# Fourteen matmuls on constants between the first and the second transposes of x

## The chip, the cores and the metric

The kernel runs on one core of one Trainium2 chip. The metric is the device time of one execution in microseconds (us). A core has five engines, each with a queue of its own that is worked off in order: TensorE (PE in the profile, with its weight loads as PEld), VectorE (DVE), ScalarE (ACT), GpSimd (POOL) and SyncE (SP), which only issues DMAs here. They wait for each other through semaphores.

## The reference

The reference is an encoder of two layers on 512 tokens of width 2048, with 16 learned tokens put ahead. Layer 0 is attention (16 query heads, 8 key and value heads, head width 128), layer 1 is gated linear attention in chunks. Each layer norms its input, projects it, mixes, gates, projects back, norms again and adds to the stream. For the change only the beginning matters:

```python
h = jnp.concatenate([meta, x], axis=1)
...
y = rmsnorm(h, pre_norm[i])
...
proj = h @ w_in
q, k, v, gate = jnp.split(
    proj, [ATTN_WIDTH, ATTN_WIDTH + ATTN_KV_WIDTH, ATTN_WIDTH + 2 * ATTN_KV_WIDTH], axis=-1)
```

All of it is in float32. The kernel reaches that precision by splitting each operand into a high and a low part and adding three products: high by high, low by high, high by low.

## The kernel before

x comes in with tokens on the partitions, and the projections need it with channels there. The kernel works in 16 steps of 128 channels, k = 0 to 15. `start_k(k)` (L441) makes one step ready: four transposes on TensorE into a PSUM tile `pt` (L444, one for each 128 tokens); on ScalarE the high part `uh`, scaled by the norm's weight (L445); on VectorE the low part `ul` (L446), which needs `uh`; and on ScalarE a copy `h0` of `pt` (L449), which GpSimd writes to memory (L450). There are two `pt` buffers, so the transposes of a step wait until the copy of an earlier one is done. From k = 4 on, `start_k` also squares pieces of x for the norm's sum, on ScalarE (L463, which writes its unused result over `pt`) and on VectorE (L466). A square on VectorE reads x alone, nothing that TensorE makes.

`meta()` (L426) does the same for the 16 learned tokens: 16 small transposes (L429), a copy (L431), a product (L434), a split.

`group` (L172) is the first projection: one key head and two query heads, each in two halves of 264 tokens, so six PSUM tiles. They are called `pp` (three of them) and `g3`, `g4`, `g5`. For every k each tile takes three matmuls: L155 (`uh` by `whi`), L156 (`ul` by `whi`), L157 (`uh` by `wlo`). For k = 0, 1, 2 it does the first half of the tokens first, then the second half, since that one needs the learned tokens.

The weights come as blocks of 128 x 1024 (`wraw`), two buffers in all, and are split by `weights` and `split` (L131 to L133): the high part `whi` on ScalarE (L132), the low part `wlo` on VectorE (L133). The first two blocks come in pieces; one piece is split on GpSimd (L384, L385). The next blocks are loaded by SyncE as a buffer comes free (L150). SyncE's queue also brings x: four pieces of 128 channels, then two of 256 and two of 512 (L369).

Ahead of it all stand 13 matmuls of a tile of ones by itself, on the tile `warm` (L401).

The order in which the engines' instructions stand is not the order of the code. A scheduler places them by estimates of when each can run, except for instructions held by `pin`, which keep their place among each other.

Of the kernel before, what the change touches and what calls it, by code (L numbers as in the profile page):

```python
# [19 lines left out]
P = 128  # L20
# [62 lines left out]
def hybrid_encoder(  # L83
# [6 lines left out]
    V, A, G, PE = nc.vector, nc.scalar, nc.gpsimd, nc.tensor  # L90
    clk = Clock()
    pin = tc.keep_in_program_order
# [26 lines left out]
    ones_r = const.tile([P, P], F32R, name="ones_r")  # L119
# [11 lines left out]
    def split(hi, lo, src):  # L131
        A.copy(hi, src)  # L132
        V.tensor_tensor(lo, src, hi.bitcast(F32), op=ALU.subtract)  # L133
# [234 lines left out]
    def load_x(c, n):  # L368
        nc.sync.dma_start(out=xt[:, :, c:c + n], in_=x_v[:, :, c:c + n])  # L369
# [9 lines left out]
    def split_w(i, k, m):  # L379
        raw, n = ((raw0, P), (raw1, 256))[i]  # L380
        c = slice(k * n, (k + m) * n)
        hi, lo = [t[:, c] for t in unit0[i, 0]]
        if i and k == 0:
            G.tensor_copy(hi, raw[:, c])  # L384
            G.tensor_tensor(lo, raw[:, c], hi.bitcast(F32), op=ALU.subtract)  # L385
        else:
            split(hi, lo, raw[:, c])
# [14 lines left out]
    accs, banks = [], []  # L402
# [18 lines left out]
    def load_rows():  # L421
        for src, r0, n in vec:
            flat = src.rearrange("a b c -> (a b c)") if len(src.shape) == 3 else src.rearrange("a b -> (a b)")
            nc.gpsimd.dma_start(out=rows[r0:r0 + n, :], in_=flat.rearrange("(r p) -> r p", p=P))

    def meta():  # L426
        mt = ps_t.tile([P, 512], F32, tag="t", name="mt")[:, :KT * META].rearrange("p (k m) -> p k m", m=META)
        for k in range(KT):
            PE.transpose(mt[:, k], xm[:, k * P:(k + 1) * P], ident[:META, :META])  # L429
        h0m = sp.tile([P, KT, META], F32, name="h0m")  # L430
        V.tensor_copy(h0m, mt)  # L431
        nc.gpsimd.dma_start(out=h0_d[:, :, SEQ:].rearrange("k p m -> p k m"), in_=h0m)
        um = sp.tile([P, KT, META], F32, name="um")
        V.tensor_tensor(um, h0m, pre0.unsqueeze(2).broadcast_to([P, KT, META]), op=ALU.mult)  # L434
        split(uh[:, :, SEQ:], ul[:, :, SEQ:], um)
# [5 lines left out]
    def start_k(k):  # L441
        pt = ps_t.tile([P, 512], F32, tag="t", name="pt")
        for t in range(4):
            PE.transpose(pt[:, t * P:(t + 1) * P], xs[t][:, k * P:(k + 1) * P], ident)  # L444
        A.activation(uh[:, k, :SEQ], pt, AF.Copy, scale=pre0[:, k:k + 1])  # L445
        V.scalar_tensor_tensor(ul[:, k, :SEQ], pt, pre0[:, k:k + 1], uh[:, k, :SEQ].bitcast(F32),  # L446
                               op0=ALU.mult, op1=ALU.subtract)
        h0 = s2.tile([P, SEQ], F32, tag="h0", name="h0", bufs=6)
        A.copy(h0, pt)  # L449
        nc.gpsimd.dma_start(out=h0_d[k][:, :SEQ], in_=h0)  # L450
        if k >= 4 and todo:
            square(*todo.pop(0), pt)
        if k >= 8 and todo:
            square(*todo.pop(0), None)
# [15 lines left out]
    def start(k, part):  # L470
        if part == 1:
            return
        for at, c, n in ((1, 768, 256), (3, 1024, 512), (6, 1536, 512)):
            if at == k:
                load_x(c, n)
        if k == 0:
            split_w(0, 0, 4)
            start_k(0)
            split_w(1, 0, 2)
            split_w(1, 2, 2)  # L480
        if k == 4:
            load_rows()
        if k == 2:
            split_w(0, 4, 4)
            meta()
        if k + 1 < KT:
            start_k(k + 1)
    group([(w_in0, 2048, P), (w_in0, 0, 256)], accs, start, 0, halves=3,
          units={(i, 0): [t.rearrange("p (k n) -> p k n", n=n) for t in unit0[i, 0]] for i, n in ((0, P), (1, 256))})
    ct = ps_t.tile([P, 512], F32, tag="t", name="ct")  # L490
# [1082 lines left out]
```

## Time and profile before

| | us |
|---|---|
| three runs | 1771.58, 1776.51, 1779.26 |
| median | 1776.51 |
| profiled execution | 1775.28 |
| its span, first to last instruction | 1773.4 |
| busy VectorE | 1150.9 |
| busy ScalarE | 991.6 |
| busy GpSimd | 389.0 |

The span leaves out 1.9 us around the instructions. Busy times say which engine is the fullest; what a change in one place is worth is read from the waits in that place. In the timelines below, a row has the start, the duration, the engine, the line, the operation, what it writes and reads (out<-in), the shapes, and in brackets how long the engine stood idle before it and what ended that. A row about DMA has the size and the median time from issue to landing.

### The profile page before, as it was taken

To read this page: it belongs to the slowest core of one execution; us is meant where nothing else is said; L and a number is where in the kernel's file an instruction comes from. 1 tells how busy PE (TensorE), PEld (TensorE's weight loads), DVE (VectorE), ACT (ScalarE), POOL (GpSimd) and SP (SyncE) were. 2 spreads that over 40 slices of the span, in tenths; PEclk is the share of its full clock that TensorE was granted. 3 is DMA by queue.
4 is the path that set the end of the run, shared out by engine and by line. 5 is a ranking of instruction groups with operands and counts; after the bars stand their busy time and mean duration, and the time that the engine had idled before them with its cause. 6 is when DMAs were issued, how large, how long until landed. Compare 5 with 4: busy or idle time off the path is not lost.

```text
span 1773.4 us, 31460 instructions
## 1 busy us (share of the span) xinstructions
PE 1733.7 (98%) x12379; PEld 1630.9 (92%) x12379; DVE 1150.9 (65%) x1799; ACT 991.6 (56%) x2032; POOL 389.0 (22%) x495
## 2 busy tenths in 40 slices
PE   8999999999999999999999999999999999999998
PEld 8999999999999999999999999998788889888886
DVE  5867775566566656786756976667677676763224
ACT  5545445666666665744457445447677685853222
POOL 3103201356456545331141001110010100000000
PEclk9999999999999999999999999999999999999999
DMA  8444434233333334464376344445333332444333
GB/s 255 139 126 133 129 120 125 77 112 109 85 107 100 109 85 110 151 198 121 110 244 176 117 138 120 120 118 143 84 112 93 102 96 78 123 126 175 95 95 130
DMA packets 273347, 220.98 MB, mean 125 GB/s; under 512 B 13324, under 2 KB 243408, under 8 KB 272672
## 3 DMA queue, kind: packets, MB, share of 16 engines
q1 hardware_dynamic: 253920, 158.76, 31.5%
q0 software_dynamic: 19280, 60.23, 10.3%
q8 instruction: 97, 1.59, 0.4%
q14 instruction: 50, 0.41, 0.1%
HBM read 177.92 MB, written 34.53 MB: 120 GB/s over the span
## 4 chain that ended last, share of the span: by engine, by line
PE 56%; DVE 4%; ACT 4%; DMA 2%; issue 1%; POOL 0%; DVEq 0%; POOLq 0%; ACTq 0%
PE pp L155 7%; PE pp L157 7%; PE pp L156 7%; PE pp L242 3%; PE pp L241 3%; PE pp L243 3%; PE f L1485 3%; PE f L1483 3%; PE f L1484 2%; PE px L243 2%; PE px L241 2%; PE px L242 2%; ACT whi L132 1%; DVE wlo L133 1%; PE o L1311 1%
## 5 line engine op out<-in xcount | busy, mean ns | idle before, releaser
L155 PE MATMUL pp<-uh,whi 128*128 128x264 f32 (+1 forms) x1744 | 549.1, 315 | 0.4 <-ACT y L888 0.3
L157 PE MATMUL pp<-uh,wlo 128*128 128x264 f32 (+1 forms) x1744 | 539.6, 309 | 1.4 <-DVE wlo L133 1.1
L156 PE MATMUL pp<-ul,whi 128*128 128x264 f32 (+1 forms) x1744 | 539.0, 309 | 2.1 <-DVE ul L446 2.1
L133 DVE TENSOR_TENSOR wlo<-wraw,whi 128x1024 fp32r<-128x1024 f32 (+1 forms) x222 | 282.5, 1273 | 234.0 <-ACT whi L132 233.3
L132 ACT CAST whi<-wraw 128x1024 fp32r<-128x1024 f32 (+1 forms) x222 | 231.3, 1042 | 273.7 <-PE f L1485 83.4
L157 PEld LDWEIGHTS pp<-uh,wlo 128*128 128x128 f32 x1744 | 329.1, 189 | 18.9 <-DVE wlo L133 1.6
L155 PEld LDWEIGHTS pp<-uh,whi 128*128 128x128 f32 x1744 | 329.1, 189 | 17.0 <-ACT uh L445 0.5
L156 PEld LDWEIGHTS pp<-ul,whi 128*128 128x128 f32 x1744 | 329.6, 189 | 16.0 <-DVE ul L446 2.6
L132 ACT CAST whi<-x 128x1024 fp32r<-128x1024 f32 x82 | 86.1, 1050 | 121.0 <-PE pp L242 70.9
L133 DVE TENSOR_TENSOR wlo<-x,whi 128x1024 fp32r<-128x1024 f32 x82 | 102.7, 1262 | 44.5 <-ACT whi L132 44.4
L241 PE MATMUL px<-uh,whi 128*128 128x264 f32 x320 | 91.3, 285 | 0.0
L243 PE MATMUL px<-uh,wlo 128*128 128x264 f32 x320 | 91.1, 285 | 0.0
L709 ACT ACTIVATE pn<-s,mx 128x528 f32<-128x528 f32 (+1 forms) x72 | 50.5, 701 | 72.1 <-DVE mx L706 72.1
L242 PE MATMUL px<-ul,whi 128*128 128x264 f32 x320 | 90.7, 283 | 0.0
L706 DVE TENSOR_REDUCE mx<-s 128x1 f32<-128x528 f32 (+1 forms) x72 | 50.8, 706 | 55.6 <-PE s L703 55.1
L1485 PE MATMUL f<-whi,ul 128*128 128x512 f32 x192 | 75.6, 394 | 0.0
L1483 PE MATMUL f<-whi,uh 128*128 128x512 f32 x192 | 75.6, 394 | 0.0
L1484 PE MATMUL f<-wlo,uh 128*128 128x512 f32 x192 | 75.4, 393 | 0.0
L314 POOL DMA_DIRECT2D qs<-qw x96 | 48.0, 506 | 98.7 <-ACT sq L308 76.6
L726 DVE TENSOR_TENSOR pl<-pT,ph 128x512 fp32r<-128x512 f32 (+1 forms) x80 | 47.5, 594 | 25.5 <-ACT ph L725 24.9
L242 PEld LDWEIGHTS px<-ul,whi 128*128 128x128 f32 x320 | 60.2, 188 | 0.0
L243 PEld LDWEIGHTS px<-uh,wlo 128*128 128x128 f32 x320 | 60.2, 188 | 0.0
(491 smaller groups left out, 4539.8 us busy)
## 6 DMA issues: line engine op xcount, KB each, us to landing
wraw<-in_gla_w_in_dram SPq DMA_DIRECT2D x77, 512.0 KB, 4.0
wraw<-in_attn_w_in_dram SPq DMA_DIRECT2D x75, 512.0 KB, 4.0
wraw<-in_gla_w_out_dram SPq DMA_DIRECT2D x32, 512.0 KB, 3.9
wraw<-in_attn_w_out_dram SPq DMA_DIRECT2D x23, 512.0 KB, 4.6
x<-in_attn_w_in_dram SPq DMA_DIRECT2D x19, 512.0 KB, 4.4
x<-in_gla_w_in_dram SPq DMA_DIRECT2D x19, 512.0 KB, 4.1
qs<-qw POOLq DMA_DIRECT2D x96, 66.0 KB, 3.5
g_d<-y POOLq DMA_DIRECT2D x20, 264.0 KB, 2.4
```

Source lines behind the costliest of these rows:

```text
L132: A.copy(hi, src)
L133: V.tensor_tensor(lo, src, hi.bitcast(F32), op=ALU.subtract)
L155: PE.matmul(ps, wh, uh[:, k, a:b], start=first, stop=False)
L156: PE.matmul(ps, wh, ul[:, k, a:b], start=False, stop=False)
L157: PE.matmul(ps, wl, uh[:, k, a:b], start=False, stop=last)
L241: PE.matmul(ps, w[0][:, k], bh[:, k], start=k == 0 and not more, stop=False, skip_group_check=more)
L242: PE.matmul(ps, w[0][:, k], bl[:, k], start=False, stop=False, skip_group_check=more)
L243: PE.matmul(ps, w[1][:, k], bh[:, k], start=False, stop=k == KH - 1, skip_group_check=more)
L706: V.reduce_max(mx, s, axis=AX.XY, negate=True)
L1483: PE.matmul(ps, uh[:, k, ts], wh[:, kk], start=(k == 0), stop=False)
L1484: PE.matmul(ps, uh[:, k, ts], wl[:, kk], start=False, stop=False)
L1485: PE.matmul(ps, ul[:, k, ts], wh[:, kk], start=False, stop=(k == KT - 1))
```

## The change

Behind the first step of `start_k`, fourteen matmuls of the tile of ones by itself are put, into the tile `g3` of the projection (`accs[-2]` after its sort). The first matmul of the projection on that tile starts its sum anew, so nothing of theirs is kept. `pin` keeps them in their place.

```diff
@@ -483,6 +483,9 @@
         if k == 2:
             split_w(0, 4, 4)
             meta()
+        if k == 0:
+            for _ in range(14):
+                pin(PE.matmul(accs[-2][0][:, :P], ones_r, ones_r, start=True, stop=True))
         if k + 1 < KT:
             start_k(k + 1)
```

On TensorE they stand between the transposes of k = 0 and those of k = 1. They also change the scheduler's estimates, and with them the order on ScalarE, VectorE and GpSimd up to about k = 7. SyncE's order is the same, and so are all orders behind that. Three places matter.

VectorE at k = 2, before. `ul` from `pt_196` is that of k = 2; the `junk` rows are squares of x, `h0m` and `um` belong to the learned tokens.

```order
L133 TENSOR_TENSOR wlo_121<-wraw_118,whi_120 128x512
L446 SCALAR_TENSOR_TENSOR ul_89<-pt_196,pre0_155,uh_88 128x512
L431 COPY h0m_234<-mt_217 128x256
L466 SCALAR_TENSOR_TENSOR junk_428,ssq_158<-xt_116 128x512
L434 TENSOR_TENSOR um_237<-h0m_234,pre0_155 128x256
L466 SCALAR_TENSOR_TENSOR junk_471,ssq_158<-xt_116 128x512
L446 SCALAR_TENSOR_TENSOR ul_89<-pt_241,pre0_155,uh_88 128x512
```

The same place now, where `pt_190` is k = 1, `pt_210` is k = 2 and `pt_255` is k = 3:

```order
L133 TENSOR_TENSOR wlo_121<-wraw_118,whi_120 128x512
L446 SCALAR_TENSOR_TENSOR ul_89<-pt_190,pre0_155,uh_88 128x512
L466 SCALAR_TENSOR_TENSOR junk_442,ssq_158<-xt_116 128x512
L466 SCALAR_TENSOR_TENSOR junk_485,ssq_158<-xt_116 128x512
L446 SCALAR_TENSOR_TENSOR ul_89<-pt_210,pre0_155,uh_88 128x512
L431 COPY h0m_248<-mt_231 128x256
L466 SCALAR_TENSOR_TENSOR junk_516,ssq_158<-xm_117 16x512
L434 TENSOR_TENSOR um_251<-h0m_248,pre0_155 128x256
L466 SCALAR_TENSOR_TENSOR junk_547,ssq_158<-xt_116 128x512
L446 SCALAR_TENSOR_TENSOR ul_89<-pt_255,pre0_155,uh_88 128x512
```

The first two squares of x have moved ahead of the `ul` of k = 2.

ScalarE at k = 5, before. `pt_288` is k = 4, `pt_329` is k = 5, `pt_358` is k = 6; `wraw_448` is the block of weights for k = 8 to 15 of the key head.

```order
L132 CAST whi_318<-wraw_317 128x1024
L445 ACTIVATE uh_88<-pt_329,pre0_155 128x512
L132 CAST whi_449<-wraw_448 128x1024
L449 COPY h0_336<-pt_329 128x512
L463 ACTIVATE pt_329,ssq_158<-xt_116 128x512
L445 ACTIVATE uh_88<-pt_358,pre0_155 128x512
```

And now, where `pt_255`, `pt_302`, `pt_343` and `pt_372` are k = 3 to 6, and `wraw_462` is the same block of weights:

```order
L132 CAST whi_332<-wraw_331 128x1024
L449 COPY h0_262<-pt_255 128x512
L449 COPY h0_309<-pt_302 128x512
L463 ACTIVATE pt_302,ssq_158<-xt_116 128x512
L132 CAST whi_463<-wraw_462 128x1024
L445 ACTIVATE uh_88<-pt_343,pre0_155 128x512
L449 COPY h0_350<-pt_343 128x512
L445 ACTIVATE uh_88<-pt_372,pre0_155 128x512
```

The split of that block has moved ahead of the `uh` of k = 5, and two copies of h have moved behind the split of the block ahead of it.

VectorE at k = 5, before:

```order
L466 SCALAR_TENSOR_TENSOR junk_601,ssq_158<-xt_116 128x512
L466 SCALAR_TENSOR_TENSOR junk_632,ssq_158<-xt_116 128x512
L446 SCALAR_TENSOR_TENSOR ul_89<-pt_329,pre0_155,uh_88 128x512
L466 SCALAR_TENSOR_TENSOR junk_663,ssq_158<-xm_117 16x512
L133 TENSOR_TENSOR wlo_450<-wraw_448,whi_449 128x1024
L446 SCALAR_TENSOR_TENSOR ul_89<-pt_358,pre0_155,uh_88 128x512
```

And now:

```order
L466 SCALAR_TENSOR_TENSOR junk_615,ssq_158<-xt_116 128x512
L466 SCALAR_TENSOR_TENSOR junk_646,ssq_158<-xt_116 128x512
L466 SCALAR_TENSOR_TENSOR junk_677,ssq_158<-xm_117 16x512
L133 TENSOR_TENSOR wlo_464<-wraw_462,whi_463 128x1024
L446 SCALAR_TENSOR_TENSOR ul_89<-pt_343,pre0_155,uh_88 128x512
L446 SCALAR_TENSOR_TENSOR ul_89<-pt_372,pre0_155,uh_88 128x512
```

The low part of the same weights has moved ahead of the `ul` of k = 5.

## The prediction

> **What bounds the kernel now.** I read the busy times first, then the table of clock and busy time by window, then what TensorE (PE) waits for in the first 45 us, then the timeline of each engine there.
>
> ```profile
> span 1773.4 us, 31460 instructions
> ...
> PE 1733.7 (98%) x12379; PEld 1630.9 (92%) x12379; DVE 1150.9 (65%) x1799; ACT 991.6 (56%) x2032; POOL 389.0 (22%) x495
> ```
>
> PE is busy for 98% of the span, so whatever delays PE at the start should reach the end nearly whole. Everything the change touches lies before 45 us: behind that, all engines have the same instructions in the same order. What follows is therefore a sum in single microseconds on 1773.4.
>
> ```profile
> 1.39 3.03 PE L401 MATMUL warm<-ones_r 128*128 128x128 f32 x13 [1.39 <-DVE ones_r L120]
> 4.57 1.12 PE L444 MATMUL pt<-ident,xt 128*128 128x128 f32 x4
> 8.25 1.09 PE L444 MATMUL pt<-ident,xt 128*128 128x128 f32 x4 [2.56 <-DMA xt<-in_x_dram]
> 11.40 0.59 PE L157 MATMUL pp<-uh,wlo 128*128 128x264 f32 x1 [0.32 <-POOL wlo L385]
> 12.00 0.42 PE L157 MATMUL g<-uh,wlo 128*128 128x264 f32 x1
> 12.22 0.42 PE L155 MATMUL pp<-uh,whi 128*128 128x264 f32 x1
> 13.50 0.28 PE L157 MATMUL pp<-uh,wlo 128*128 128x264 f32 x1
> 13.62 0.28 PE L155 MATMUL pp<-uh,whi 128*128 128x264 f32 x1
> ```
>
> This is PE's timeline: start, duration, what it is, and in brackets the idle time before it. The gap of 2.56 us, between the transposes of k = 0 and of k = 1, is where the new matmuls go. The second thing to see is the spacing: two 264-column matmuls start 0.22 us apart at 12.2 and 0.12 us apart at 13.5. PE runs at half clock until about 13.5 in spite of the 13 matmuls at the start.
>
> ```profile
> 10.05:13.46 3.41, 3.09 (x14) 1.00 1.05 261
> 3.22:6.63 3.41, 2.47 (x11) 1.00 1.04 308
> 177.30:180.71 3.41, 1.57 (x13) 1.00 0.10 29
> 180.71:184.13 3.42, 3.42 (x18) 0.50 0.43 125
> 494.74:498.15 3.41, 1.72 (x16) 1.00 0.50 148
> ```
>
> Here the columns are the window, its length, PE's busy time, the granted clock, and DMA. (The clock records begin at 13.46; for the two earlier windows the spacing above is the evidence, not the 1.00.) A window with 3.09 of 3.41 us busy ends half clock; one with 2.47 does not. Later a window with 1.57 busy is followed by one at 0.50, one with 1.72 is not. A window at half clock that is full of matmuls costs half of 3.41, about 1.7 us.
>
> **The change: the 14 matmuls themselves.** Thirteen of the same kind took 3.03 us at half clock, the spacing 0.21. Fourteen take 3.0 us, from the last first transpose (about 5.5) to 8.5. The second transposes began at 8.25, so they move by 0.25 at most, and by nothing if the clock rises on the way. PE is then busy from 1.39 to 8.5, so a full 3.41 us window lies in it wherever the windows fall: full clock comes at 4.8 to 8.2 instead of 13.5.
>
> What that buys: nothing up to 11.40, since the matmul there waits for GpSimd's `wlo` (L385), which no PE work delays or hastens. From 11.40 to 13.5 PE issues eight matmuls and four transposes at half clock; at full clock that is about 1.0 us less. So PE comes to the k = 2 matmuls 1.0 us earlier. The cost of the matmuls is nothing; the cover is the 2.56 us wait for x and the wait for L385.
>
> **The change: the order.** The diff's other effect is the reordering shown above, and there I find the time.
>
> ```profile
> 15.99 0.28 PE L156 MATMUL pp<-ul,whi 128*128 128x264 f32 x1
> 14.26 0.75 DVE L446 SCALAR_TENSOR_TENSOR ul<-pt,pre,uh 128x512 fp32r<-128x512 f32 x1 [1.47 <-ACT uh L445]
> 15.97 0.68 DVE L466 SCALAR_TENSOR_TENSOR junk<-xt 128x512 f32<-128x512 f32 x1
> 16.91 0.68 DVE L466 SCALAR_TENSOR_TENSOR junk<-xt 128x512 f32<-128x512 f32 x1
> L369 SPq DMA_DIRECT2D xt<-in_x_dram x1: 1695/1695/1695, 6.0 to 6.0; - x1
> DMA to landing us min/median/max: 9.2/9.2/9.2
> ```
>
> *k = 2.* `ul` of k = 2 was made at 14.26, ahead of two squares of x. Now the squares stand ahead of it, and they read the part of x that was issued at 6.0 and landed 9.2 later, at 15.2. So `ul` starts at about 15.3 + 2 x 0.76 = 16.8 and ends at 17.6, and PE's L156 moves from 15.99 to 17.6. The 1.0 us gained is gone here, with another 1.6. This alone would not yet hurt, because of the next stop.
>
> ```profile
> 26.44 0.37 PE L155 MATMUL pp<-uh,whi 128*128 128x264 f32 x1
> 28.50 0.39 PE L156 MATMUL pp<-ul,whi 128*128 128x264 f32 x1 [1.69 <-DVE ul L446]
> 30.70 0.60 PE L444 MATMUL pt<-ident,xt 128*128 128x128 f32 x4
> 32.01 0.39 PE L156 MATMUL pp<-ul,whi 128*128 128x264 f32 x1 [0.40 <-DVE ul L446]
> 34.17 0.60 PE L444 MATMUL pt<-ident,xt 128*128 128x128 f32 x4
> 34.73 0.29 PE L156 MATMUL pp<-ul,whi 128*128 128x264 f32 x1
> 36.80 0.60 PE L444 MATMUL pt<-ident,xt 128*128 128x128 f32 x4
> 24.11 0.69 ACT L445 ACTIVATE uh<-pt,pre 128x512 fp32r<-128x512 f32 x1 [1.56 <-PE pt L444]
> 28.31 1.05 ACT L132 CAST whi<-wraw 128x1024 fp32r<-128x1024 f32 x1 [3.50 <-DMA wraw<-in_attn_w_in_dram]
> 26.35 0.69 DVE L466 SCALAR_TENSOR_TENSOR junk<-xt 128x512 f32<-128x512 f32 x1 [2.54 <-DMA xt<-in_x_dram]
> 27.70 0.74 DVE L446 SCALAR_TENSOR_TENSOR ul<-pt,pre,uh 128x512 fp32r<-128x512 f32 x1
> 29.39 1.23 DVE L133 TENSOR_TENSOR wlo<-wraw,whi 128x1024 fp32r<-128x1024 f32 x1 [0.34 <-ACT whi L132]
> ```
>
> *k = 5.* Today `uh` of k = 5 is made at 24.11, then ScalarE waits 3.50 us for a block of weights, first needed at k = 8. `ul` of k = 5 waits on VectorE behind squares that wait for the last of x, and PE loses 1.69 us. In the new order the split of those weights stands ahead of both: on ScalarE `whi` ahead of `uh`, on VectorE `wlo` ahead of `ul`. The load's landing becomes the bound:
> - `whi` 28.31 to 29.36; `uh` to 30.05; `wlo` 29.39 to 30.62; `ul` 30.62 to 31.37; L156 of k = 5 at 31.43, against 28.50: **+2.93**.
> - PE gets there in time: from L156 of k = 2 to L155 of k = 5 took 26.44 - 15.99 = 10.45 us, so from 17.6 it arrives at 28.1, and at about 29 with the waits for the next `ul` and `um`. It then waits some 2.4 us. That slack also hides half clock behind the k = 2 stall.
> - Part comes back. From L156 of k = 5 to the next transposes takes 30.70 - 28.50 = 2.20, so they run at 33.63. Before, 1.31 us passed from there to L156 of k = 6, with a stall; undisturbed it is 34.73 - 34.17 = 0.56. ScalarE frees the transposes' buffer by 33.2 and `ul` of k = 6 is done by 33.4 (same durations, counted on from 31.37), so PE does not stall: 34.19 against 32.01. The next transposes come 36.80 - 34.73 = 2.07 later, at 36.26 against 34.17: **+2.1 us**, kept from there on, since later loads start when a buffer comes free and move along.
>
> The least certain term is the landing.
>
> ```profile
> 12.38 0.51 SPq L369 DMA_DIRECT2D xt<-in_x_dram  x1
> 13.01 1.72 SPq L150 DMA_DIRECT2D wraw<-in_attn_w_in_dram  x1
> xt<-in_x_dram SPq DMA_DIRECT2D x1, 1024.0 KB, 13.9
> wraw<-in_attn_w_in_dram SPq DMA_DIRECT2D x1, 512.0 KB, 15.2
> h_d<-h POOLq DMA_DIRECT2D x1, 256.0 KB, 6.5
> ```
>
> The load was issued at 13.01 and landed 15.2 later, at 28.2, behind the x load that landed at 26.3. SyncE's queue keeps its order. It can be issued 0.6 earlier, but DMA is full, so that gains nothing. It cannot land before 26.3, which gives +0.1. Two writes of h of 256 KB move behind 22.5 and may compete with it; 512 KB at the 261 GB/s above is 2.0 us, which gives +4.1 as the other end. I take 28.2, the load's own row.
>
> The profiled execution took 1775.28 us; with +2.1 it is 1777.4. The median of the three runs, 1776.51, stands 1.2 above it, so the forecast is **1778.6**. The three runs lie 4.9 below to 2.8 above their median. A difference under 0.5% (8.9 us) cannot be told from none here, so I call this no measurable change.
>
> **Rivals.** *Faster: the early clock reaches the end.* The 1.0 us stays and PE ends at 1775.5. It needs `ul` of k = 5 by 27.4, so the weights by 24.2. For it: the 0.12 spacing; against: the x load ahead in the same queue landed at 26.3. Chance 0.08.
>
> *No effect.* The load lands with x at 26.3, which leaves +0.1: 1776.6. For it: on ScalarE two copies of h now come later, and so do their writes. Against: the same bytes go through a full DMA. Chance 0.12. *The change doesn't do what it says:* the clock stays at half up to 13.5. Then the k = 2 stall comes as before, since a load ends it, and the time is the forecast's; this is a part of its chance.
>
> *One window at half clock after the k = 5 stall.* PE idles for some 1.9 us in the 2.4 before 31.43 (L155 lies between). The window from 177.30 shows that 1.57 busy of 3.41 is too little, the one from 494.74 that 1.72 is enough; 1.5 us would be busy here if the whole gap fell into one window, which about a third of the positions do. It costs 1.7 more: 1780.3. Chance 0.22. [...]
>
> *Slower by over 0.5%: half clock holds on.* With +2.1 it needs four more windows at 1.7 us before PE is dense again. The place is 17 to 31 us. Against it: a full window ends it at once (180.71 to 184.13 was alone), and 2.4 us of slack at 31 covers the first. Chance 0.03: 1786.
>
> **How the numbers follow.** The forecast has 0.55, with 1776.6 to 1780.6 by the landing's bounds. The range takes in the faster rival and the one window, and the runs' own scatter of some 3 us: 1773.0 to 1783.0. Faster by over 0.5%: 0.02; slower: 0.04; within: 0.94.
>
> **What would show it.** In the new profile: matmuls 0.12 apart from 11.40 on (or a fall back to 0.22 after the stall at 15 to 17.6, which changes nothing later); L156 of k = 2 near 17.6 waiting for `ul`; on ScalarE `whi` at 28 with `uh` straight behind it; L156 of k = 5 near 31.4; the transposes of k = 8 near 36.3. Wrong would be a PE that passes k = 5 before 28.5, or any difference in the spans behind 45 us.

## The result, and the profile after

The kernel with the change takes 1776.66 us (median of 22 runs, 1773.5 to 1783.99); the kernel before took 1772.59 in the 22 runs beside them (1768.65 to 1779.26). The ratio is 1.0027, with a 95% interval of 1.0017 to 1.0038: slower by a quarter of a per cent, inside the half per cent that was called no change. The profiled execution took 1779.16 us.

First the page of the changed kernel: the span, and the busy times of the engines.

```profile
span 1777.3 us, 31489 instructions
...
PE 1738.0 (98%) x12393; PEld 1635.4 (92%) x12393; DVE 1148.4 (65%) x1799; ACT 992.0 (56%) x2032; POOL 388.7 (22%) x495
```

The span is 3.9 us longer than before, and PE is busy for 4.3 us more. PE has 14 instructions more (12393 against 12379).

**The start.** PE's timeline of the changed kernel; the columns are start, duration, engine, line, operation, out<-in, shapes, and the idle time before with what ended it.

```profile
5.34 3.23 PE L488 MATMUL g<-ones_r 128*128 128x128 f32 x14
8.36 1.07 PE L444 MATMUL pt<-ident,xt 128*128 128x128 f32 x4
9.46 0.42 PE L156 MATMUL pp<-ul,whi 128*128 128x264 f32 x1
9.68 0.42 PE L157 MATMUL pp<-uh,wlo 128*128 128x264 f32 x1
11.39 0.28 PE L156 MATMUL g<-ul,whi 128*128 128x264 f32 x1
11.52 0.28 PE L157 MATMUL g<-uh,wlo 128*128 128x264 f32 x1
17.22 0.59 PE L156 MATMUL pp<-ul,whi 128*128 128x264 f32 x1 [2.26 <-DVE ul L446]
```

The 14 matmuls fill the old wait of 2.56 us, and the second transposes move by 0.11, from 8.25 to 8.36. But behind them the 264-column matmuls still start 0.22 us apart (9.46, 9.68). At 11.39 and 11.52 they are 0.13 apart. The clock records of this execution begin at 10.34, the end of the second window below.

```profile
3.52:6.93 3.41, 3.41 (x18) 3.25 (x17) 0.81 (x2) 1.52 (x4) 0.00 (x0) 1.00 1.02 313
6.93:10.34 3.41, 3.41 (x17) 3.30 (x16) 2.39 (x4) 2.15 (x4) 1.72 (x3) 1.00 1.16 278
13.76:17.17 3.41, 1.21 (x14) 0.97 (x12) 2.06 (x6) 0.00 (x0) 0.84 (x2) 1.00 1.06 371
17.17:20.58 3.41, 3.36 (x15) 3.36 (x16) 2.46 (x7) 1.57 (x3) 1.74 (x2) 0.50 1.06 384
```

In this table by window the first column after the length is PE's busy time; the granted clock comes behind POOL (ahead of 10.34 it isn't a record). From 3.52 to 6.93 PE is busy for the whole window (3.41 of 3.41), and half clock goes on up to 10.34, by the 0.22 us between the matmuls at 9.46 and 9.68. Behind the stall at k = 2 (13.76 to 17.17, 1.21 busy) stands one window at half clock (17.17 to 20.58, 0.50).

**k = 5.** ScalarE, VectorE and PE of the changed kernel, in this order:

```profile
28.11 1.05 ACT L132 CAST whi<-wraw 128x1024 fp32r<-128x1024 f32 x1 [4.10 <-DMA wraw<-in_attn_w_in_dram]
29.06 0.68 ACT L445 ACTIVATE uh<-pt,pre 128x512 fp32r<-128x512 f32 x1
29.19 1.23 DVE L133 TENSOR_TENSOR wlo<-wraw,whi 128x1024 fp32r<-128x1024 f32 x1 [0.66 <-ACT whi L132]
30.33 0.75 DVE L446 SCALAR_TENSOR_TENSOR ul<-pt,pre,uh 128x512 fp32r<-128x512 f32 x1
31.13 0.39 PE L156 MATMUL pp<-ul,whi 128*128 128x264 f32 x1 [0.95 <-DVE ul L446]
33.31 0.60 PE L444 MATMUL pt<-ident,xt 128*128 128x128 f32 x4
35.93 0.60 PE L444 MATMUL pt<-ident,xt 128*128 128x128 f32 x4
54.84 0.60 PE L444 MATMUL pt<-ident,xt 128*128 128x128 f32 x4
```

The chain is the forecast one: the load lands, `whi`, `uh`, `wlo`, `ul`, L156. The last two rows are the transposes of k = 8 (34.17 before) and of k = 15. In the kernel before, the latter stand here:

```profile
53.08 0.60 PE L444 MATMUL pt<-ident,xt 128*128 128x128 f32 x4
```

So at k = 8 and at k = 15 the changed kernel is 1.76 us behind. The other 2.1 us of the 3.9 come later. The windows at half clock show one part of them; the first three rows are the changed kernel, the last three the kernel before.

```profile
181.01:184.42 3.41, 3.41 (x17) 3.41 (x17) 3.41 (x4) 0.00 (x0) 0.88 (x1) 0.50 0.53 154
385.81:389.22 3.41, 3.41 (x17) 3.40 (x18) 3.07 (x6) 1.92 (x6) 1.80 (x4) 0.50 0.76 226
679.36:682.77 3.41, 3.41 (x18) 3.41 (x17) 1.76 (x4) 1.39 (x4) 0.46 (x1) 0.50 0.65 163
```

```profile
385.81:389.22 3.41, 3.41 (x30) 3.41 (x30) 1.89 (x6) 1.99 (x7) 1.73 (x3) 1.00 0.33 83
556.18:559.59 3.41, 3.41 (x18) 3.41 (x16) 3.38 (x4) 1.17 (x3) 3.31 (x3) 0.50 0.33 120
679.36:682.77 3.41, 3.41 (x31) 3.41 (x30) 1.37 (x4) 2.05 (x8) 0.00 (x0) 1.00 0.42 131
```

In these rows PE issues 17 or 18 matmuls where the granted clock is 0.50, 30 or 31 where it is 1.00. Two such windows (385.81, 679.36) are in the changed kernel's execution only, one (556.18) in that of before only; one near 180 and one near 618 are in both. That is one more in the changed kernel, an estimated 1.7 us of lost work (half of 3.41).

### The profile page after: what moved, and what is told of

It is laid out like the page before. It is cut to its first block, busy times and chain, and to the rows that moved or that the text cites. A ratio compares the mean times of both kernels' runs of the same rounds, so it can differ in the third digit from the quotient of the medians.

```text
span 1777.3 us, 31489 instructions
## 1 busy us (share of the span) xinstructions
PE 1738.0 (98%) x12393; PEld 1635.4 (92%) x12393; DVE 1148.4 (65%) x1799; ACT 992.0 (56%) x2032; POOL 388.7 (22%) x495
## 3 DMA queue, kind: packets, MB, share of 16 engines
q1 hardware_dynamic: 253920, 158.76, 31.5%
q8 instruction: 97, 1.59, 0.4%
## 4 chain that ended last, share of the span: by engine, by line
PE 81%; DVE 6%; ACT 6%; DMA 4%; issue 2%; POOL 1%; SPq 0%; DVEq 0%; ACTq 0%; POOLq 0%
PE pp L155 11%; PE pp L156 11%; PE pp L157 11%; PE pp L243 4%; PE pp L241 4%; PE pp L242 4%; PE px L243 3%; PE px L241 3%; PE px L242 3%; PE f L1488 2%; PE f L1486 2%; PE f L1487 2%; ACT whi L132 2%; DMA wraw<-in_attn_w_in_dram 2%; DVE wlo L133 2%
## 5 line engine op out<-in xcount | busy, mean ns | idle before, releaser
L155 PE MATMUL pp<-uh,whi 128*128 128x264 f32 (+1 forms) x1744 | 549.0, 315 | 0.9 <-ACT uh L445 0.6
L156 PE MATMUL pp<-ul,whi 128*128 128x264 f32 (+1 forms) x1744 | 539.0, 309 | 3.2 <-DVE ul L446 3.2
L157 PE MATMUL pp<-uh,wlo 128*128 128x264 f32 (+1 forms) x1744 | 539.7, 309 | 1.7 <-DVE wlo L133 1.1
L132 ACT CAST whi<-wraw 128x1024 fp32r<-128x1024 f32 (+1 forms) x222 | 231.2, 1042 | 269.9 <-PE f L1488 83.4
L157 PEld LDWEIGHTS pp<-uh,wlo 128*128 128x128 f32 x1744 | 329.3, 189 | 19.1 <-DVE wlo L133 1.6
L156 PEld LDWEIGHTS pp<-ul,whi 128*128 128x128 f32 x1744 | 329.8, 189 | 17.2 <-DVE ul L446 3.8
L155 PEld LDWEIGHTS pp<-uh,whi 128*128 128x128 f32 x1744 | 329.4, 189 | 17.1 <-ACT uh L445 0.8
L132 ACT CAST whi<-x 128x1024 fp32r<-128x1024 f32 x82 | 86.1, 1050 | 121.4 <-PE pp L242 69.0
```

What stands on the lines that cost most here:

```text
L155: PE.matmul(ps, wh, uh[:, k, a:b], start=first, stop=False)
L156: PE.matmul(ps, wh, ul[:, k, a:b], start=False, stop=False)
L157: PE.matmul(ps, wl, uh[:, k, a:b], start=False, stop=last)
```

## The experiments

The theory: the matmuls cost nothing; the order at k = 5 delays PE; what comes behind 60 us is no effect of the change, but depends on how many windows at half clock fall into an execution. The rivals: the matmuls themselves do it, or the change brings windows at half clock later on.

A helper in these kernels only fixes an order: `order_behind(a, b)` queues `a` behind `b` on their engine, without a semaphore. `mark` keeps the instructions: `hi` and `lo` of the split of the weights for k = 8 to 15, `uh` and `ul` of a step, and `sq` for a square (piece q of x, tile t). One table holds all readings; the sections below refer to it. "whi" is the start of that block's `whi`, as soon as its load has landed and ScalarE is free; "k = 15" the start of its transposes; "windows" those at half clock after k = 15, without PE's run-out at the end. Ratios are to runs of the kernel before beside them.

| kernel | whi | L156 of k = 5 | k = 15 | span | windows | ratio (95%) |
|---|---|---|---|---|---|---|
| before | 28.31 | 28.50 | 53.08 | 1773.4 | 3 | |
| before_again | 28.55 | 29.16 | 54.42 | 1774.0 | 3 | 0.9997 (0.9985 to 1.0009) |
| changed | 28.11 | 31.13 | 54.84 | 1777.3 | 4 | 1.0027 (1.0017 to 1.0038) |
| after_again | 27.85 | 30.87 | 54.59 | 1770.3 | 2 | 1.0007 (0.9992 to 1.0023) |
| after_third | 28.36 | 31.37 | 56.67 | 1775.4 | 2 | 1.0001 (0.9988 to 1.0014) |
| after_fourth | 27.31 | 30.33 | 54.05 | 1772.6 | 2 | 0.9997 (0.998 to 1.0014) |
| order_k5 | 28.29 | 31.30 | 54.43 | 1770.0 | 2 | 1.0009 (0.9995 to 1.0023) |
| order_only | 28.41 | 31.42 | 54.76 | 1769.5 | 0 | 0.9995 (0.9979 to 1.0010) |
| pad_order | 27.18 | 27.85 | 52.32 | 1772.1 | 3 | 0.9998 (0.9988 to 1.0008) |
| pad_free7 | | 28.92 | 53.35 | 1767.8 | 0 | 1.0013 (0.9996 to 1.0029) |
| free7 | | 28.04 | 53.10 | 1773.7 | 2 | 0.9995 (0.9979 to 1.0010) |
| wide_order | 28.05 | 29.37 | 53.53 | 1767.0 | 1 | 0.9991 (0.9979 to 1.0003) |
| wide_free | 28.79 | 30.43 | 54.03 | 1766.7 | 0 | 1.0002 (0.9986 to 1.0017) |

### The order without the matmuls

order_k5 is the kernel before, with one part of the new order: the split of the weights ahead of `uh` and `ul` of k = 5.

```diff
                     units[i, k // nk] = weights(src[:, k:k + nk, c0:c0 + n], ahead)
+                    if halves == 3 and (i, k) == (0, 8):
+                        order_behind(mark["uh", 5], mark["hi"])
+                        order_behind(mark["ul", 5], mark["lo"])
```

> The kernel before, without the 14 matmuls; only the split of the key head's weights for k = 8 to 15 is queued ahead of uh and ul of k = 5, as the change has it. If that order is the cost: L156 of k = 5 at 31.1 to 31.5 us in place of 28.5, the transposes of k = 8 at 35.6 to 36.3 in place of 34.17, and a time 1.5 to 4 us above before (ratio 1.001 to 1.0025). If the matmuls or the squares at k = 2 are the cost: L156 of k = 5 no later than 29.5 and a ratio of 1.000.

order_only has the squares of x ahead of `ul` as well, at k = 2 and k = 3.

```diff
+    AHEAD_OF = {(1, 0): 2, (1, 2): 2, (2, 1): 3}
...
+            if (q, t) in AHEAD_OF:
+                order_behind(mark["ul", AHEAD_OF[q, t]], mark["sq", q, t])
```

> The kernel before, without the 14 matmuls, with both moves: squares of x ahead of ul of k = 2, and the split of the weights ahead of uh and ul of k = 5. If the order is the cost: L156 of k = 2 at 17.0 to 17.7, L156 of k = 5 at 31.1 to 31.5, the transposes of k = 8 at 35.6 to 36.3, ratio as that of the change (1.0017 to 1.0038). If the matmuls are the cost: ratio 1.000 to 1.001.

ScalarE and PE of order_k5 (L138, L161 and L162 are L132, L155 and L156 of the kernel before):

```profile
28.29 1.04 ACT L138 CAST whi<-wraw 128x1024 fp32r<-128x1024 f32 x1 [5.71 <-DMA wraw<-in_attn_w_in_dram]
29.97 0.52 PE L161 MATMUL pp<-uh,whi 128*128 128x264 f32 x2 [2.59 <-ACT uh L454]
31.30 0.39 PE L162 MATMUL pp<-ul,whi 128*128 128x264 f32 x1 [0.33 <-DVE ul L455]
```

Without a single new matmul, L156 of k = 5 stands at 31.30, and at 31.42 with both parts of the order. In all six executions with this order, of four changed kernels and these two, L156 follows the start of `whi` by 3.01 or 3.02 us (28.29 to 31.30, 28.11 to 31.13). In five of them the landing of the load sets that start. order_only is the exception, and not the changed kernel's order in full: on VectorE the copy `h0m` still stands ahead of the squares and waits 3.78 us for PE, so L156 of k = 2 comes at 19.93 (17.0 to 17.7 was expected). At k = 5 its load had landed at 27.3, ScalarE was at a copy and a square until 28.41, and PE itself arrives at about 31.4.

The times don't show the cost. order_k5, at 1.0009 where 1.001 to 1.0025 was expected, may have it or not (0.9995 to 1.0023). order_only missed: 1.0017 to 1.0038 was expected, and its interval ends at 1.0010. Taken together, their 24 runs stand 0.5 us above the 35 of the kernel before beside them, give or take 1.8.

### The matmuls without the order

pad_order is the changed kernel, with both engines held to the old order at the two places.

```diff
+    BEHIND = {(1, 0): 2, (1, 2): 2, (2, 1): 4, (2, 3): 4}
...
+                        order_behind(mark["hi"], mark["uh", 5])
+                        order_behind(mark["lo"], mark["ul", 5])
...
+            if (q, t) in BEHIND:
+                order_behind(mark["sq", q, t], mark["ul", BEHIND[q, t]])
```

> The 14 matmuls, with the order of before at both places: the squares behind ul of k = 2, the split of the weights behind uh and ul of k = 5. If the order is the cost: L156 of k = 2 at 14.5 to 15.5, L156 of k = 5 at 28.2 to 28.8, the transposes of k = 8 within 0.5 us of 34.17, ratio 0.999 to 1.001. If the matmuls are the cost: ratio 1.0017 to 1.0038 as in the change.

before_again is the kernel before, unchanged.

> The kernel before as it is, for a second trace and for what the comparison makes of no difference. Every theory: ratio 1.000 within its interval, the transposes of k = 8 within 0.4 us of 34.17. It shows by how much two executions of the same program drift apart behind 45 us, and whether the windows of the clock lie at the same place in the program.

ScalarE, VectorE and PE of pad_order:

```profile
25.09 0.69 ACT L454 ACTIVATE uh<-pt,pre 128x512 fp32r<-128x512 f32 x1 [1.75 <-PE pt L453]
27.18 1.05 ACT L138 CAST whi<-wraw 128x1024 fp32r<-128x1024 f32 x1 [1.40 <-DMA wraw<-in_attn_w_in_dram]
27.06 0.73 DVE L455 SCALAR_TENSOR_TENSOR ul<-pt,pre,uh 128x512 fp32r<-128x512 f32 x1
27.85 0.39 PE L162 MATMUL pp<-ul,whi 128*128 128x264 f32 x1
```

`uh` is made before the load lands, `ul` beside `whi`, and L156 comes 0.67 us behind the start of `whi` in place of 3.02. The matmuls stand at 5.34 to 8.4 as in the changed kernel, and no cost of theirs shows: k = 15 is reached at 52.32, the earliest of all. A part of that is the load, which landed a microsecond earlier than in the kernel before (`whi` at 27.18 against 28.31). Up to k = 6 PE is later than before, not earlier (transposes at 27.07 against 26.09), and L156 of k = 2, at 16.96, misses the range of 14.5 to 15.5: GpSimd's `wlo` let L157 start at 11.85 in place of 11.40, and half clock lasted to 14.78 (matmuls at 14.41 and 14.63 start 0.22 us apart, those at 14.82 and 14.95 0.13). Whether the matmuls have a part in that, this run doesn't show; the wait at k = 5 covers it. The time is that of before, 0.9998 (0.9988 to 1.0008), so at the start the order makes the wait, while in the time no difference shows.

The repeat of the kernel before is later than the first one by 1.36 at k = 8 (35.53, where 34.17 within 0.4 was expected) and by 1.34 at k = 15, with the same instructions. Its table by window shows why:

```profile
26.91:30.32 3.41, 1.17 (x9) 1.17 (x10) 3.28 (x8) 1.74 (x3) 0.00 (x0) 1.00 0.39 123
30.32:33.73 3.41, 3.41 (x18) 3.41 (x17) 1.28 (x2) 2.20 (x5) 1.08 (x2) 0.50 0.64 195
```

Its wait for `ul` of k = 5 (2.48 us, up to 29.16) fell nearly whole into one window (1.17 of 3.41 us busy), and the next had half clock (0.50). So at k = 15 one execution differs from the next of the same kernel by as much as the change makes.

### The waits taken away

pad_free7 and free7, with and without the new matmuls, put off the split and the last squares until behind k = 7, so that nothing which waits for a load stands ahead of `uh` and `ul` of k = 5 and 6.

```diff
+    BEHIND = {(1, 0): 2, (1, 2): 2, (2, 1): 4, (2, 3): 4, (3, 0): 7, (3, 2): 7, (3, 4): 7}
...
+                        order_behind(mark["hi"], mark["uh", 7])
+                        order_behind(mark["lo"], mark["ul", 7])
```

> The 14 matmuls, with the squares of x and the split of the weights for k = 8 to 15 queued behind what TensorE waits for (squares of the second quarter of x behind ul of k = 2, of the third behind ul of k = 4, of the fourth and the split behind uh and ul of k = 7). If loads that stand ahead in ScalarE's and VectorE's queues are what stalls TensorE at k = 5: no stall over 0.5 us between 18 and 35 us, the transposes of k = 8 at 30.5 to 32.0 in place of 34.17, those of k = 15 at 50.0 to 51.5, ratio 0.997 to 0.9995. If the stall has another cause: k = 8 at 33 or later, ratio 0.9995 to 1.002.

> The same order without the 14 matmuls. If the matmuls buy about 1 us up to k = 2 that this order lets through: the transposes of k = 15 0.5 to 1.2 us later than in the run with them, ratio 0.998 to 1.000. If they buy nothing: both alike within 0.3 us.

The stall at k = 5 is gone in both, and k = 8 is reached at 33.62 and 32.74 (34.17 before). But k = 15 comes at 53.35 and 53.10, like the kernel before. From k = 8 to k = 15 the changed kernel took 54.84 - 35.93 = 18.91 us; these took 19.73 and 20.36. What was saved ahead of k = 8 was given back behind it. PE's timeline of free7 names two of the places:

```profile
41.67 0.66 PE L453 MATMUL pt<-ident,xt 128*128 128x128 f32 x4 [0.40 <-ACT pt L472]
50.93 0.39 PE L162 MATMUL pp<-ul,whi 128*128 128x264 f32 x1 [0.40 <-DVE ul L455]
```

They are waits for ScalarE and VectorE, on which the postponed work now stands. Neither kernel is faster than before, and the expectation for pad_free7 missed: k = 8 came at 33.62 in place of 30.5 to 32.0, and the ratio is 1.0013 in place of 0.997 to 0.9995. These are the numbers that had been named for another cause of the stall, but no stall is left; PE works without a gap there (its transposes at 25.74, 28.36, 30.98 and 33.62, 2.62 us a step). So at k = 8 the stall of before is worth 0.55 to 1.43 us (34.17 against 33.62 and 32.74), not two or three. With the matmuls and without, k = 15 is alike within the 0.3 us that had been named for matmuls that buy nothing.

### Wider matmuls

Why did the clock not rise? The new matmuls have 128 columns and start 0.213 us apart, and PE counts as busy. The 264-column matmuls of the projection start 0.22 us apart at the same half clock (9.46 and 9.68 in the changed kernel), with twice the columns. wide_order is pad_order with the 13 and the 14 matmuls 264 columns wide; wide_free also puts the last squares of x behind `ul` of k = 5.

```diff
+    wide_r = sp.tile([P, HALF], F32R, name="wide_r")
+    V.tensor_copy(wide_r, wide)
...
-        PE.matmul(warm[:, :P], ones_r, ones_r, start=True, stop=True)
+        PE.matmul(warm[:, :HALF], ones_r, wide_r, start=True, stop=True)
...
-                pin(PE.matmul(accs[-2][0][:, :P], ones_r, ones_r, start=True, stop=True))
+                pin(PE.matmul(accs[-2][0], ones_r, wide_r, start=True, stop=True))
```

> The order of before at k = 2 and k = 5, with 13 and 14 matmuls that are 264 columns wide in place of 128. Theory (the clock follows the share of a 3.41 us window in which columns stream; 128 columns started 0.213 apart at half clock stream for half the time, 264 columns started 0.22 apart for all of it): the clock rises at 4.8 to 8.4, the matmuls behind the rise stand about 0.11 to 0.12 apart, the transposes of k = 1 start at 8.3 or before, those of k = 2 at about 11.7, L156 of k = 5 as early as 28 or before. Rival (it follows busy time, and something else than width keeps it at half clock: ones as data, one single tile): spacing 0.22 throughout, rise at 10 to 15 as with narrow ones. On the time both expect little, since what PE gains before k = 5 waits there for x and weights: ratio 0.998 to 1.001.

> The wide matmuls, and on VectorE and ScalarE each ul and uh of k = 2 to 5 ahead of squares and of the split of the weights of k = 8 to 15. Theory: clock at 4.8 to 8.4, L156 of k = 5 at 28 or before, transposes of k = 8 at 32 to 33.5 and of k = 15 at 52 to 53.4; as the best of both, ratio 0.998 to 1.000. Rival (what is put off on VectorE comes back as a wait at k = 6 to 8): L156 of k = 5 early, k = 15 at 53.5 or later.

PE's timeline, two rows of wide_order, then three of wide_free:

```profile
5.92 2.57 PE L503 MATMUL g<-wide_r,ones_r 128*128 128x264 f32 x14
29.37 0.39 PE L162 MATMUL pp<-ul,whi 128*128 128x264 f32 x1 [3.04 <-DVE ul L459]
```

```profile
5.42 1.93 PE L503 MATMUL g<-wide_r,ones_r 128*128 128x264 f32 x14
8.46 0.63 PE L457 MATMUL pt<-ident,xt 128*128 128x128 f32 x4 [1.11 <-DMA xt<-in_x_dram]
12.10 0.59 PE L163 MATMUL pp<-uh,wlo 128*128 128x264 f32 x1 [1.27 <-POOL wlo L398]
```

The same number of matmuls, twice as wide, takes less time (2.57 and 1.93 us against 3.23). The clock rose early in both: the four transposes behind the 13 take 1.11 us in wide_order and 0.66 in wide_free (1.11 in the changed kernel), those behind the 14 take 0.60 and 0.63 (1.07 there). The window from 3.85 in wide_order is as busy as the one from 3.52 in the changed kernel, 3.41 us each: that part of the theory stands in these executions.

What it expected further on is a miss. In wide_order PE comes early to k = 5 and then waits 3.04 us, since on VectorE `ul` stands behind squares that wait for the last of x, which VectorE has only at 26.50. In wide_free the time saved goes into waits for x (1.11) and for GpSimd (0.86 and 1.27), and half clock stands again from 11.50 to 21.74 (0.50 in the windows from 11.50 and from 18.33, matmuls 0.22 us apart at 15.10 and 15.32 between them). Both reach k = 15 later than pad_order. The early full clock bought nothing in these two executions, as the loads and the other engines set the start. wide_order has the lowest ratio, 0.9991, but its interval takes in 1.

### The changed kernel again

Three more comparisons of the changed kernel, unchanged, on other occasions.

> The changed kernel as it is, beside the two below on one chip. If the order at the start is all of the cost: transposes of k = 15 at 54.4 to 55.4 us (53.08 and 54.42 in the two traces of before), and a ratio of 1.0005 to 1.002, below the 1.0027 first measured, the rest of which is chance in where half-clock windows fall later. If the change costs something of its own behind 45 us: ratio again 1.0017 to 1.0038.

> The changed kernel once more. Theory (the order at the start costs 1 to 2 us, the rest of the first result was how many windows at half clock fell into those runs): L156 of k = 5 at 30.8 to 31.5, transposes of k = 15 at 54.4 to 54.9, ratio 1.0003 to 1.0015. Rival (the change itself brings more windows at half clock later): ratio 1.002 to 1.004 and a granted clock lower than that of the kernel before by 0.001 or more.

> The changed kernel once more, to settle what its first comparison (ratio 1.0027, mean granted clock 0.9955) held beyond the 1 to 2 us of the start. Theory (the rest was how many windows at half clock fell into those runs, which the change does not set): ratio 1.0000 to 1.0016, mean granted clock of the runs 0.9960 to 0.9968 as in the second and third comparison. Rival (the change brings more windows at half clock later in the program): ratio 1.002 or more and a mean clock of 0.9956 or less. In both, L156 of k = 5 starts at 30.8 to 31.5.

The ratios are 1.0007, 1.0001 and 0.9997. The mean granted clock of their runs was 0.9964, 0.9964 and 0.9968, against 0.9955 in the first comparison. One window at half clock in 1775 us lowers the mean by 1.7 / 1775 = 0.00096 (1.7 being half of 3.41), so by this estimate the first runs had about one more of them each. A straight line through all 262 runs with a recorded clock, each kernel with its own level, gives 1.71 us (95%: 1.48 to 1.93) for each 0.001. So the rival, that the change brings such windows, would have had to show again, and did not. A mean as low also comes without the change: the 17 runs of the kernel before beside after_fourth have 0.9957, those beside the other runs 0.9962 and 0.9966. L156 of k = 5 in after_fourth, 30.33, misses the range of 30.8 to 31.5: its load landed earlier, and 27.31 + 3.02 gives the 30.33. Its ratio, 0.9997, lies just below the expected 1.0000 to 1.0016.

after_third shows the case that had been given 0.22, one window at half clock behind the stall at k = 5:

```profile
28.83:32.24 3.41, 1.25 (x8) 1.05 (x9) 1.89 (x2) 2.05 (x4) 0.01 (x1) 1.00 0.10 31
32.24:35.65 3.41, 3.41 (x18) 3.41 (x17) 0.75 (x1) 2.21 (x6) 1.07 (x2) 0.50 0.69 243
```

Its k = 15 stands at 56.67 (54.4 to 54.9 was expected), 1.8 to 2.6 behind the three other executions. It was one of four.

## Why the prediction was right, point by point

- **The matmuls cost nothing, and move the second transposes by 0.25 at most**: the move is shown, 0.11. No cost shows either: pad_order is at k = 15 before all others, with the help of an early load, and its time can't be told from that of before (0.9988 to 1.0008).
- **Full clock at 4.8 to 8.2**: wrong, and the step of the mechanism that failed. It came at 10.34 (13.46 in the kernel before), and in after_fourth later than in the kernel before: matmuls of 264 columns at 18.95 and 19.17 still start 0.22 us apart there. The step took busy time as what raises the clock, from a window of the kernel before with 3.09 of 3.41 busy that had full clock behind it (10.05) and one with 2.47 that had not (3.22). The changed kernel's window from 3.52 has 3.41 busy and had not. It cost the forecast nothing, because the gain of 1.0 us that hung on it was counted as lost at k = 2 in any case; the rival that the clock stays at half had been given the forecast's time for that reason. wide_order, in the old order, fits this reason: with the early clock PE waits 3.04 us at k = 5.
- **k = 2: L156 from 15.99 to 17.6 behind two squares**: right, 17.22. x landed a little earlier than the 15.2 taken; the first square starts at 15.07.
- **k = 5: L156 from 28.50 to 31.43**: right, 31.13. The load landed before 28.11 in place of 28.2, and the steps behind it took 3.02 us in place of the 3.12 worked out. PE waited less than the 1.9 us estimated, 0.60 and 0.95, and kept its clock (1.00 in the window from 27.41, with 2.17 us busy, and in the one behind it). Without the order the delay is gone (pad_order), with the order alone it is there (order_k5).
- **+2.1 us at k = 8, kept from there on**: +1.76, kept to k = 15. "Kept" holds for a comparison of two profiled executions only. The kernel before reached k = 15 at 53.08 and 54.42, the changed one at 54.84, 54.59, 56.67 and 54.05: the two overlap.
- **The time, 1778.6**: measured 1776.66, inside the range, and in part by luck. The forecast stood on the median of three runs, 1776.51, which lies 3.9 above the median of all 22 (1772.59), and the first measured difference, +4.07, is nearly twice the +2.1. The two errors partly offset each other. The prediction also held that a difference under 0.5% cannot be told from none; with 22 runs on each side the interval was 0.2% wide and left 1 out. Two of its small sums are inexact, with nothing resting on them: a landing together with x gives +0.2 and not +0.1 (2.1 less 1.9), and four windows at half clock give 1785.4 and not 1786.
- **The size of the difference**: +2.1 was forecast. The first comparison gave +4.07 in the medians, the three later ones together +0.7 in the means, give or take 1.2 (36 runs against 75). All of them, 58 runs of the changed kernel against 132 of before, give +1.8, give or take 1.0. In the first comparison both sides lay apart from their other runs: the kernel before had a mean of 1772.8 (1774.4 in its 110 other runs), the changed one 1777.5 (1775.0 in its 36 other runs). By the straight line above, at an equal clock, the changed kernel stands 1.3 us above the kernel before, give or take 0.7; order_k5 1.4 above, order_only 0.5 above and pad_order 0.6 below, each give or take 1.4. (The 22 runs of before in the first comparison have no recorded clock and are not in that line.) So a cost of one to two microseconds is likely and fits the order; that the order makes all of it is not shown in the times, and the three later comparisons alone do not exclude zero. Why the first runs had a lower clock stays open; nothing in the change is shown to do it.
- **"Any difference in the spans behind 45 us" would be wrong**: there was one, and it is the windows at half clock. The prediction had them in the runs' scatter of 3 us, without a name. Span less k = 15 in the table gives the part behind the start: 1712.6 to 1714.7 with no window, 1719.6 to 1720.3 with three, 1722.5 with four, about 2 us for each. With two it lies between 1715.6 and 1720.6, so they are not all of the scatter.

## What to carry to other kernels

A scheduler that places by estimates answers an addition in one queue with a new order in others; here the delay was there, where an instruction that waits for a load came to stand ahead of one that did not. Follow such a chain from its first instruction behind the load: from there on it repeated to a hundredth of a microsecond. Where loads set the start, as here, a faster engine only waited longer (3.04 us at k = 5 in wide_order, 1.69 in the kernel before); and before a difference of 2 us in 1775 is explained, count the windows at half clock in each execution.

## What the runs showed of the hardware

**A window fully busy with 128-column matmuls had half clock behind it, one with 264-column matmuls full clock.** In the changed kernel the window from 3.52 is busy for 3.41 of 3.41 us, mostly with 128-column matmuls 0.213 us apart and transposes; the 264-column matmuls behind it still start 0.22 us apart (9.46, 9.68). In wide_order the window from 3.85 is busy for 3.41 us as well, mostly with 264-column matmuls and four transposes; behind it, matmuls of 264 columns start 0.12 us apart (8.89, 9.01). Two windows at half clock that were less busy had full clock behind them: the one from 10.05 in the kernel before, with 3.09 us (0.12 apart at 13.50 and 13.62), and the one from 617.92 in the changed kernel, with 2.73 us (1.00 from 621.33 on). So busy time doesn't part these four. At the spacings measured, 128 columns in 0.213 us are 601 columns in a microsecond and 264 in 0.22 are 1200, an estimate from the starts of the matmuls. The early rise of the two wide kernels was expected beforehand and came in both; at how many columns the clock rises was not shown.

**A wait of 2.48 us had half clock behind it, one of 3.04 us had not.** The windows of before_again (26.91, wait of 2.48 up to 29.16) and after_third (28.83, waits of 1.80 up to 30.04 and 0.94 up to 31.37) were followed by half clock (0.50) with 1.17 and 1.25 of 3.41 us busy. Two longer waits were not, and each lay across the border of two windows: 2.59 us in order_k5 (up to 29.97) and 3.04 in wide_order (up to 29.37). First the two windows of order_k5, then those of wide_order:

```profile
25.79:29.20 3.41, 1.59 (x14) 1.35 (x12) 2.09 (x6) 0.91 (x1) 0.00 (x0) 1.00 0.60 210
29.20:32.62 3.42, 2.32 (x17) 2.11 (x17) 2.55 (x3) 2.60 (x7) 0.46 (x1) 1.00 0.20 54
```

```profile
24.33:27.74 3.41, 2.00 (x17) 1.80 (x16) 2.06 (x7) 0.10 (x1) 0.00 (x0) 1.00 1.11 354
27.74:31.15 3.41, 1.78 (x14) 1.78 (x15) 2.67 (x6) 2.81 (x5) 0.54 (x1) 1.00 0.10 33
```

In the kernel before, the windows at full clock with 0.78, 1.23 and 1.57 us busy (614.21, 552.77, 177.30) had half clock behind them, the one with 1.72 (494.74) had not. In the changed kernel those with 1.21, 1.29, 1.44, 1.47 and 1.59 (13.76, 382.40, 675.95, 614.50, 177.60) had it; order_k5's with 1.59 (25.79) had not, so with the same busy time both happened. Where the windows lie changed from one execution to the next of the same kernel (27.11 in before, 26.91 in before_again; 27.41 in the changed kernel, 28.83 in after_third). A wait of about the same length (2.48 in before_again, 2.59 in order_k5) had a window at half clock behind it in one execution, an estimated 1.7 us more (half of 3.41), and none in another.
